# The first input tile of a pooling kernel is loaded by two transfers instead of one

## The chip, the cores and the metric

The kernel runs on one core of a Trainium2 chip. The core has compute engines with instruction streams of their own: VectorE (DVE in the profile), ScalarE (ACT), GpSimd (POOL) and TensorE (PE, not used here), and SyncE (SP), which issues transfers. Transfers are carried out by 16 DMA engines. SBUF is the memory on the core, with 128 partitions; the input and the output lie in the chip's main memory (HBM). The metric is the device time of one execution in microseconds (us).

## The reference

The input is 32 x 256 rows of 4096 float32 numbers. Each row is cut into 256 windows of 16 neighbours, and the output holds the mean of each window:

```python
batch, channels, length = x.shape          # 32, 256, 4096
for i in range(output_size):               # 256
    start = int(i * length / output_size)
    end = int((i + 1) * length / output_size)
    result[:, :, i] = np.mean(x[:, :, start:end], axis=-1)
```

That is 134.2 MB read and 8.4 MB written.

## The kernel before

The 8192 rows are worked through in 16 tiles. A tile gives each of the 128 partitions 4 rows that lie one behind the other in HBM, so 16,384 numbers or 64 KB; a tile is 8.39 MB. For the first 15 tiles partition p owns rows 60p to 60p+59 and takes 4 of them at a time (`x_many`); the last tile has 512 rows of its own, 4 to a partition (`x_last`). Within a tile the numbers of a partition are seen as `cells` = 1024 windows of `window` = 16.

The pool `inpool` has two buffers for the tile `xin`, so tile t+2 goes into the buffer of tile t. `res_many` holds the results of the first 15 tiles, `res_last` those of the last.

For each tile, in this order in the program:

- L66: SP issues the load of the whole tile, one transfer over 128 partitions. It waits until the work on the tile that had this buffer before is done.
- In the last tile only, L68: SP issues the store of `res_many`, 7680 KB, behind the last load. It waits for L80 of tile 14.
- L69: POOL takes the second half of the windows (`m` = 512 of 1024 and up) and adds the upper 8 numbers of each to the lower 8.
- L74: DVE sums the first half of the windows, 16 numbers each.
- L77: DVE sums the second half, 8 numbers each, after L69.
- L80: ACT multiplies the 1024 sums by 1/16 in place.

After the loop, L85 stores `res_last`, 512 KB. Each engine works through its own instructions in program order, and the framework puts in the waits that the data ask for. All transfers, loads and stores, are issued by SP and stand in one queue.

Of the kernel before, what the change touches and what calls it, by code (L numbers as in the profile page):

```python
# [1 line left out]

# [4 lines left out]


@with_exitstack
def kernel(  # L10
    ctx: ExitStack,
    tc: tile.TileContext,
    x: bass.AP,
    output_size: int,
    out: bass.AP,
):

    nc = tc.nc
    F32 = mybir.dt.float32
    X = mybir.AxisListType.X

    batch, channels, length = x.shape
    ob, oc, olen = out.shape
    assert ob == batch and oc == channels and olen == output_size
    assert length % output_size == 0
    window = length // output_size  # L30
    hw = window // 2
    inv_w = 1.0 / float(window)

    P = nc.NUM_PARTITIONS
    R = 4
    rows = batch * channels
    assert rows % (P * R) == 0
    ntiles = rows // (P * R)
    many = (ntiles - 1) * R
    cells = R * output_size  # L40
    m = cells // 2
    cols = R * length

    xr = x.rearrange("b c l -> (b c) l")
    orow = out.rearrange("b c o -> (b c) o")
    x_many = xr[0 : P * many, :].rearrange("(p r) l -> p (r l)", p=P, r=many)
    o_many = orow[0 : P * many, :].rearrange("(p r) o -> p (r o)", p=P, r=many)
    x_last = xr[P * many :, :].rearrange("(p r) l -> p (r l)", p=P, r=R)
    o_last = orow[P * many :, :].rearrange("(p r) o -> p (r o)", p=P, r=R)

    padpool = ctx.enter_context(tc.tile_pool(name="padpool", bufs=1))
    padpool.tile([P, 32], F32, name="pad")
    inpool = ctx.enter_context(tc.tile_pool(name="inpool", bufs=2))
    respool = ctx.enter_context(tc.tile_pool(name="respool", bufs=1))
    res_many = respool.tile([P, (ntiles - 1) * cells], F32, name="res_many")
    res_last = respool.tile([P, cells], F32, name="res_last")

    for t in range(ntiles):
        last = t == ntiles - 1
        xin = inpool.tile([P, cells, window], F32, name="xin")  # L60
        if last:
            res, base, src = res_last, 0, x_last
        else:
            res, base = res_many, t * cells
            src = x_many[:, t * cols : (t + 1) * cols]
        nc.sync.dma_start(out=xin.rearrange("p o w -> p (o w)"), in_=src)  # L66
        if last:
            nc.sync.dma_start(out=o_many, in_=res_many[:, :])  # L68
        nc.gpsimd.tensor_add(  # L69
            out=xin[:, m:cells, 0:hw],  # L70
            in0=xin[:, m:cells, 0:hw],
            in1=xin[:, m:cells, hw:window],
        )
        nc.vector.reduce_sum(  # L74
            out=res[:, base : base + m], in_=xin[:, 0:m, :], axis=X
        )
        nc.vector.reduce_sum(  # L77
            out=res[:, base + m : base + cells], in_=xin[:, m:cells, 0:hw], axis=X
        )
        nc.scalar.mul(  # L80
            out=res[:, base : base + cells],
            in_=res[:, base : base + cells],
            mul=inv_w,
        )
    nc.sync.dma_start(out=o_last, in_=res_last[:, :])  # L85


# [1 line left out]
_INS = ['x', 'output_size']  # L89
_OUTS = [((32, 256, 256), 'float32')]  # L90

_NUMBERS = {'output_size': 256}


# [26 lines left out]
```

## Time and profile before

| | us |
|---|---|
| median of 3 runs | 334.89 (334.88 to 334.91) |
| the profiled execution | 335.07 |
| its span, first to last instruction | 333.3 |
| DVE busy | 209.7 (63%) |
| POOL busy | 139.7 (42%) |
| ACT busy | 18.2 (5%) |
| a load (L66), median from issue to landing | 25.3 |
| the first load, from issue to landing | 21.7 |
| the store of `res_many` (L68), from issue to landing | 23.7 |
| the store of `res_last` (L85), from issue to landing | 4.9 |

The span is what the profile's own rows cover; what lies around it is in the time of the execution but not in the rows. The profile's page gives the busy time of each engine, the packets of the DMA queue, the chain of waits that ended last, and the costliest groups of instructions with the idle time ahead of them and what ended it. The trace can be asked for any stretch of the span: busy time of each engine, the share of the 16 DMA engines, and the rate. In those stretches a DMA packet is counted where it starts, with its whole duration and its bytes; a stretch much shorter than a packet can therefore show a share above 1, or 0 while engines are at work.

### The profile page before, as it was taken

What the parts mean: (1) busy time and instruction counts of PE and PEld (TensorE: products, weight loads), DVE (VectorE), ACT (ScalarE), POOL (GpSimd) and SP (SyncE); (2) the same over time, 40 slices, a digit from 0 to 9 for tenths busy, and PEclk for the clock granted to TensorE, in tenths of its full rate; (3) what the DMA queues carried; (4) which work ended last, traced back from release to release, by engine and by line L of the source; (5) the groups of instructions that cost most, each with busy time, mean ns of one, the idle gap of its engine ahead of it and who ended that gap; (6) DMA issues with size and microseconds to landing.
All of it is one profiled execution on the core that took longest, in us unless ns stands there. A gap on an engine that the chain in (4) does not pass through costs nothing.

```text
span 333.3 us, 158 instructions
## 1 busy us (share of the span) xinstructions
DVE 209.7 (63%) x32; ACT 18.2 (5%) x17; POOL 139.7 (42%) x20
## 2 busy tenths in 40 slices
DVE  0039295693929568392957849294774929487491
ACT  1000101000010100001010100101010010101001
POOL 0027090643709063360907346090724519082460
DMA  9898989999898989899898989899998989898996
GB/s 378 378 503 378 503 378 472 409 401 480 378 503 378 503 378 496 385 433 448 385 496 378 503 378 503 378 472 409 401 480 378 503 378 503 378 496 385 391 442 299
DMA packets 2592, 142.61 MB, mean 428 GB/s; under 512 B 288, under 2 KB 288, under 8 KB 416
## 3 DMA queue, kind: packets, MB, share of 16 engines
q1 hardware_dynamic: 2592, 142.61, 99.1%
HBM read 134.22 MB, written 8.39 MB: 428 GB/s over the span
## 4 chain that ended last, share of the span: by engine, by line
DMA 66%; POOL 18%; DVE 11%; POOLq 3%; issue 0%; ACT 0%; SPq 0%
DMA xin<-in_x_dram 66%; POOL xin L69 18%; DVE res_many L77 9%; POOLq L116 3%; DVE res_last L77 1%; ACT res_last L80 0%; SPq L66 0%; POOLq L69 0%
## 5 line engine op out<-in xcount | busy, mean ns | idle before, releaser
L69 POOL TENSOR_TENSOR xin<-xin 128x4096 f32<-128x4096 f32 x16 | 139.5, 8717 | 182.0 <-DMA xin<-in_x_dram 182.0
L74 DVE TENSOR_REDUCE res_many<-xin 128x512 f32<-128x8192 f32 x15 | 130.3, 8686 | 107.3 <-DMA xin<-in_x_dram 107.3
L77 DVE TENSOR_REDUCE res_many<-xin 128x512 f32<-128x4096 f32 x15 | 66.3, 4420 | 2.5 <-POOL xin L69 2.3
L80 ACT ACTIVATE res_many<-res_many 128x1024 f32<-128x1024 f32 x15 | 15.8, 1056 | 289.6 <-DVE res_many L77 289.6
L74 DVE TENSOR_REDUCE res_last<-xin 128x512 f32<-128x8192 f32 x1 | 8.7, 8685 | 6.7 <-DMA xin<-in_x_dram 6.7
L77 DVE TENSOR_REDUCE res_last<-xin 128x512 f32<-128x4096 f32 x1 | 4.4, 4420 | 0.2 <-POOL xin L69 0.2
L80 ACT ACTIVATE res_last<-res_last 128x1024 f32<-128x1024 f32 x1 | 1.1, 1056 | 18.9 <-DVE res_last L77 18.9
L80 ACT ACT_TABLE_LOAD x1 | 1.3, 1283 | 0.7 <-PEq L102 0.7
L102 POOL MEMSET const-float32-0.0<- 128x1 f32 x1 | 0.1, 98 | 0.2 <-issue 0.2
L102 POOL MEMSET const-bfloat16-1.0<- 128x1 bf16 x1 | 0.1, 101 | 0.0
L102 POOL MEMSET const-uint8-127<- 128x1 uint8 x1 | 0.1, 101 | 0.0
L102 POOL MEMSET const-float32-1.0<- 128x1 f32 x1 | 0.1, 98 | 0.0
## 6 DMA issues: line engine op xcount, KB each, us to landing
out_dram<-res_many SPq DMA_DIRECT2D x1, 7680.0 KB, 23.7
out_dram<-res_last SPq DMA_DIRECT2D x1, 512.0 KB, 4.9
xin<-in_x_dram SPq DMA_DIRECT2D x16, 25.3
```

The source lines that it names most:

```text
L69: nc.gpsimd.tensor_add(out=xin[:, m:cells, 0:hw], in0=xin[:, m:cells, 0:hw], in1=xin[:, m:cells, hw:window],)
L74: nc.vector.reduce_sum(out=res[:, base : base + m], in_=xin[:, 0:m, :], axis=X)
L77: nc.vector.reduce_sum(out=res[:, base + m : base + cells], in_=xin[:, m:cells, 0:hw], axis=X)
L80: nc.scalar.mul(out=res[:, base : base + cells], in_=res[:, base : base + cells], mul=inv_w,)
L102: nc = _bacc.Bacc("TRN2", target_bir_lowering=False, num_devices=1)
L116: with _tile.TileContext(nc) as tc:
```

## The change

The load of the first tile is issued as two transfers, one behind the other on SP: partitions 0 to 15, then partitions 16 to 127. All other tiles keep one transfer over all partitions. Nothing else differs.

```diff
-        nc.sync.dma_start(out=xin.rearrange("p o w -> p (o w)"), in_=src)
+        xflat = xin.rearrange("p o w -> p (o w)")
+        for lo, hi in ((0, 16), (16, P)) if t == 0 else ((0, P),):
+            nc.sync.dma_start(out=xflat[lo:hi, :], in_=src[lo:hi, :])
```

## The prediction

> **What bounds the kernel now.** I read the page first, then the chain of waits, the timeline of the first 62 us, and stretches of the DMA record. The queue's row comes first:
>
> ```profile
> ## 3 DMA queue, kind: packets, MB, share of 16 engines
> q1 hardware_dynamic: 2592, 142.61, 99.1%
> L69 POOL TENSOR_TENSOR xin<-xin 128x4096 f32<-128x4096 f32 x16 | 139.5, 8717 | 182.0 <-DMA xin<-in_x_dram 182.0
> L74 DVE TENSOR_REDUCE res_many<-xin 128x512 f32<-128x8192 f32 x15 | 130.3, 8686 | 107.3 <-DMA xin<-in_x_dram 107.3
> ```
>
> The 16 DMA engines are busy for 99.1% of the span, and both compute engines idle for the input. The packets count themselves: 288 under 512 B are 16 (one per engine, the completion marks) for each of 18 transfers, and the remaining 2304 are 128 for each transfer. So one data packet is one partition's share, 64 KB of input, and with 16 engines each has 8 of them per tile.
>
> ```profile
> 55.05 0.02 issue
> 55.07 25.44 DMA xin<-in_x_dram
> 80.51 0.02 issue
> ```
>
> This piece of the chain, repeated every second tile, is a whole period: the load of tile t+2 is issued when L77 of tile t ends (55.07) and lands 25.44 us later, though the engines need only 19.35 us for a tile. The other 6.1 us are the rest of the load ahead of it, so the queue never runs dry. The stretches say the same:
>
> ```profile
> 2.75:22.10 19.35, 0.00 (x0) 0.00 (x0) 0.00 (x0) 1.00 1.00 434
> 22.10:41.45 19.35, 13.11 (x2) 1.06 (x1) 8.72 (x1) 1.00 1.00 434
> 273.65:293.00 19.35, 13.11 (x2) 1.06 (x1) 8.72 (x1) 1.00 1.00 434
> 312.35:331.70 19.35, 13.11 (x2) 1.06 (x1) 8.72 (x1) 1.00 0.92 395
> ```
>
> In columns: stretch, length, DVE, ACT and POOL busy, clock, DMA share, GB/s. A tile is 8.39 MB in 19.35 us, or 2.42 us per 64 KB packet and engine. The last row shows the queue still moving after the last load: the 7680 KB of `res_many` were issued at 307.51, run behind that load, and land 23.7 us later at 331.2; the last 512 KB, issued at 327.48, run behind them and land at 332.4. The chain of waits names POOL 18% and DVE 11%, but those hide under queued transfers. The end is set by the slowest DMA engine's whole list, so what that engine loses in tile 0 is added to the end one for one.
>
> The start of that list, in stretches of packet starts (GB/s times length, divided by 65,536 bytes, counts them):
>
> ```profile
> 1.60:1.70 0.10, 0.00 (x0) 0.10 (x1) 0.00 (x0) 1.00 0.00 0
> 1.70:1.80 0.10, 0.00 (x0) 0.10 (x1) 0.00 (x0) 1.00 9.91 3277
> 1.80:1.90 0.10, 0.00 (x0) 0.10 (x1) 0.00 (x0) 1.00 8.01 2621
> 1.90:2.90 1.00, 0.00 (x0) 0.11 (x1) 0.00 (x0) 1.00 1.25 459
> 2.90:4.70 1.80, 0.00 (x0) 0.00 (x0) 0.00 (x0) 1.00 0.00 0
> 4.70:5.30 0.60, 0.00 (x0) 0.00 (x0) 0.00 (x0) 1.00 4.03 1748
> 7.10:7.70 0.60, 0.00 (x0) 0.00 (x0) 0.00 (x0) 1.00 4.03 1748
> ```
>
> 5, 4 and 7 engines begin their first packet between 1.7 and 2.9 us, all 16 their second between 4.7 and 5.3, the third between 7.1 and 7.7: lockstep, 2.4 us apart. (A row counts a packet where it starts, so shares exceed 1.)
>
> **The change part by part.** *Issue.* One transfer more on SP, 0.33 us by the median of L66's sixteen, between tile 0's first issue and tile 1's. Tile 1's load then goes out some 0.33 us later, behind 19.35 us of queued work; without that cover it would cost 0.33. Nothing moves on POOL's or ACT's queue, and SP's next entry, tile 2's load, still waits for tile 0's L77.
>
> *Bytes and completion marks.* The bytes are the same. There are 16 more small packets, one per engine. The last packet of a tile and the first of the next stand 2.45 us apart (19.15 to 21.60), others 2.40 to 2.45, so a mark costs 0 to 0.05 us. I take 0.03.
>
> *Waits.* L69 and L74 of tile 0 read partitions of both pieces, so both wait for both transfers; should this take a semaphore instruction of its own, the end's rows of that kind begin at 0.017 us. Behind L69 and L74 stand only tile 0's L77 and L80 and then tile 2's load, which has 6.1 us of cover. Nothing on the end's path.
>
> *Start.* 16 packets, one per engine, could reach all engines sooner than 128. Upper bound of the gain: the second packets spread from 4.70 to 5.25 us, so if all engines ran like the earliest, 0.55 us. Lower bound: nothing, since late starters already catch up (1.0 us of spread becomes 0.55). I take 0.2 us gained.
>
> *The first piece's path.* This is the term that matters, and the trace of before does not price it. Every row shows 16 engines working at once, each through its own eight partitions; it never shows several engines sending to neighbouring partitions, and it cannot say whether 2.42 us belongs to the engine or to the strip of SBUF that it writes. The first piece puts one packet on each engine, all 16 into partitions 0 to 15. Lower bound: the engine is the limit, 2.42 us as now, cost 0. Upper bound: the strip is, with 128/16 = 8 neighbours to a strip: 16 packets in 2 strips, 8 in each, 8 x 2.42 = 19.35 us, cost +16.9. Between 16 paths and 2 I take 4 (the rows show all 16 in use only when all 128 partitions are written, so I lean to the narrow end): 4 rounds, 9.68 us, **+7.26**.
>
> *The second piece's path.* 112 partitions over 16 engines are 7 each, in whatever order. Lower bound: no collision, 7 x 2.42 = 16.9 us, cost 0. Upper bound: every engine always shares a strip with one other, since sevens do not line up with eights: 7 x 4.84 = 33.9, +16.9. I take the middle, half of the seven shared: 3.5 x 2.42 = **+8.47**. There is a floor if strips matter at all and the first piece takes 9.68 us: strips it left idle still owe their whole 8 packets, so tile 0 ends no earlier than 9.68 + 19.35, at least +9.7.
>
> [...]
>
> *Sum.* +0.03 - 0.2 + 7.26 + 8.47 = +15.6 us. On the profiled execution (span 333.3, whole run 335.07, so 1.77 around the span) that is 350.7. The median is 334.89, 0.18 lower, so the prediction is **350.5 us**, 4.7% slower. Compute keeps its cover: tile 0 lands late, tile 1's load lies behind it, and each tile's 13.3 us of work fits its 19.35 as before.
>
> **The rivals.**
>
> *No collision, no change.* The engine is the limit; 16 packets to 16 neighbours take 2.42 us. Then +0.03 - 0.2: 334.7, range 334.2 to 335.0. For it: the even lockstep, as one would see if each engine had its own speed. Against: lockstep also follows if each engine has its own strip, and before never breaks that pairing. Chance 0.20.
>
> *Faster.* The early start is worth more than I grant: all 0.55 us, and the engines' new offsets take away the last load's excess (tile 15 lands at 313.06, tile 14's at 293.09, 19.97 apart against 19.35, 0.6 us): -1.1, 333.8. It would decide only where the first piece costs under 0.5 us, so where no strip matters. For it: the DMA engines set the end, so every tenth saved at the start counts. Against: the stretches are already at 434 GB/s with no idle time to win. Chance 0.08.
>
> *Uneven shares.* The change does not use 16 engines for the short piece but 4, with 4 packets each, while the second still gives 7 to all. Then four engines have 11 packets for tile 0, 3 x 2.42 = +7.26: 342.2. The other twelve run ahead until their buffers stop them, and the end is the four's. For it: nothing in the trace fixes how 16 partitions are dealt out. Against: 128 gave exactly 8 each. Chance 0.06.
>
> *Collision* as forecast: 0.66, from its floor of +9.7 (344.6) to about +22 (357), where nearly all the second piece is shared. If the second piece collided four deep throughout, as the first, it would be 7 x 7.26 = +50.8 and the time about 393; that is in the 0.66, at 0.04, outside the range.
>
> **How the numbers follow.** What this kernel's measurement can tell from no change is about 0.2%, 0.67 us. Faster by more: 0.08; within: 0.20; slower: 0.66 + 0.06 = 0.72. The collision's own range is 344.5 to 357. Without the no-change case over 2 in 10 would be left out, so the range reaches down to 334.4 and holds all but about half of the faster case, the four-deep case and a little at its edges: **334.4 to 357**.
>
> **What would show it.** In the stretches of the DMA record: if 16 packets start by 2 us and the next only after about 11, four paths served the first piece; if the second packets start at 4.7 to 5.3 as now, none collided. Packets of 4.8 us in the stretch after that show the second piece's pairs, and their absence leaves only the floor. The wait of L74 for tile 0, 22.49 us before, should be about 38. From tile 1 on, the period should again be 19.35 us at 434 GB/s, and the loss carried unchanged to the end; a period that changes would make the one-for-one rule wrong. Unequal packet counts per stretch in tile 0 would show uneven shares. The prediction is wrong if tile 0 lands near 22.5.

## The result, and the profile after

The changed kernel takes 355.61 us (median of 4 runs, 355.17 to 356.42) against 334.88: a ratio of 1.062, 95% interval 1.061 to 1.064, so 20.7 us slower. The profiled execution took 355.50 us with a span of 353.7, 20.4 more than before. Lines have moved by two: L68 is the load, L71 POOL's addition, L76 and L79 the sums.

From the page, its head and the rows of the queue and of the compute groups that wait for input:

```profile
span 353.7 us, 161 instructions
DVE 209.7 (59%) x32; ACT 18.2 (5%) x17; POOL 139.7 (39%) x20
DMA packets 2608, 142.61 MB, mean 403 GB/s; under 512 B 304, under 2 KB 304, under 8 KB 432
q1 hardware_dynamic: 2608, 142.61, 98.8%
L71 POOL TENSOR_TENSOR xin<-xin 128x4096 f32<-128x4096 f32 x16 | 139.5, 8718 | 202.4 <-DMA xin<-in_x_dram 202.4
L76 DVE TENSOR_REDUCE res_many<-xin 128x512 f32<-128x8192 f32 x15 | 130.3, 8686 | 128.3 <-DMA xin<-in_x_dram 128.3
```

Compute is the same to 0.1 us. The 16 new packets are under 512 B (304 for 288), the marks of one transfer more; the data packets are as many as before. POOL's wait for input grew by 20.4 us (182.0 to 202.4), as much as the span. The DMA engines still count as 98.8% busy, for the 99.1% of before: they hold as many data packets for longer. The busy share does not show the loss here; the rate does, 403 GB/s for the 428 of before:

```profile
DMA packets 2592, 142.61 MB, mean 428 GB/s; under 512 B 288, under 2 KB 288, under 8 KB 416
```

The timeline has the loss in one place. Here is DVE's first sum of tiles 0, 14 and 15 before:

```profile
22.49 8.69 DVE L74 TENSOR_REDUCE res_many<-xin 128x512 f32<-128x8192 f32 x1 [22.49 <-DMA xin<-in_x_dram]
...
293.11 8.69 DVE L74 TENSOR_REDUCE res_many<-xin 128x512 f32<-128x8192 f32 x1 [6.08 <-DMA xin<-in_x_dram]
313.08 8.69 DVE L74 TENSOR_REDUCE res_last<-xin 128x512 f32<-128x8192 f32 x1 [6.69 <-DMA xin<-in_x_dram]
```

And after, the same sum of tiles 0, 1, 2, 14 and 15:

```profile
43.96 8.69 DVE L76 TENSOR_REDUCE res_many<-xin 128x512 f32<-128x8192 f32 x1 [43.96 <-DMA xin<-in_x_dram]
63.16 8.69 DVE L76 TENSOR_REDUCE res_many<-xin 128x512 f32<-128x8192 f32 x1 [5.99 <-DMA xin<-in_x_dram]
82.45 8.69 DVE L76 TENSOR_REDUCE res_many<-xin 128x512 f32<-128x8192 f32 x1 [6.07 <-DMA xin<-in_x_dram]
...
314.13 8.69 DVE L76 TENSOR_REDUCE res_many<-xin 128x512 f32<-128x8192 f32 x1 [6.09 <-DMA xin<-in_x_dram]
333.46 8.69 DVE L76 TENSOR_REDUCE res_last<-xin 128x512 f32<-128x8192 f32 x1 [6.05 <-DMA xin<-in_x_dram]
```

Tile 0 arrives at 43.96 instead of 22.49, 21.47 us late. After that the period is (314.13 - 43.96) / 14 = 19.30 us, before (293.11 - 22.49) / 14 = 19.33; that returns 0.45 us, and the last tile follows after 19.33 instead of 19.97, which returns 0.64. 21.47 - 1.09 is the 20.4 of the span.

The stretches of the changed kernel at the start (last two columns: DMA share and GB/s; a packet counts where it starts, so rate times length over 65,536 bytes is the number started, and share times length times 16 engines over that number is their mean duration):

```profile
1.60:2.20 0.60, 0.00 (x0) 0.42 (x1) 0.00 (x0) 1.00 14.20 1748
2.20:9.60 7.40, 0.00 (x0) 0.00 (x0) 0.00 (x0) 1.00 0.00 0
9.60:11.10 1.50, 0.00 (x0) 0.00 (x0) 0.00 (x0) 1.00 3.54 699
11.10:15.10 4.00, 0.00 (x0) 0.00 (x0) 0.00 (x0) 1.00 0.00 0
15.10:16.00 0.90, 0.00 (x0) 0.00 (x0) 0.00 (x0) 1.00 5.19 1165
16.00:19.80 3.80, 0.00 (x0) 0.00 (x0) 0.00 (x0) 1.00 0.00 0
19.80:20.70 0.90, 0.00 (x0) 0.00 (x0) 0.00 (x0) 1.00 3.54 1165
```

All 16 engines start in the first row (1748 GB/s x 0.60 us / 65,536 B = 16), and none starts a second packet for 7.4 us. The first packet took 14.20 x 0.60 x 16 / 16 = 8.52 us; the same sum over the first packets of before gives 2.34 x 1.30 = 3.04 (its row stands below). The second takes 3.54 x 1.50 = 5.3, the third 5.19 x 0.90 = 4.67, the fourth 3.19; the further four, by the stretches that follow, 3.7, 4.4, 4.6 and 4.6. From tile 1's second packet on all are 2.42 us again. The first packets before:

```profile
1.60:2.90 1.30, 0.00 (x0) 0.41 (x1) 0.00 (x0) 1.00 2.34 807
```

### The profile page after: what moved, and what is told of

The parts are those of the page before. It is cut to its first block, busy times and chain, and to the rows that moved or that the text cites. A ratio compares the mean times of both kernels' runs of the same rounds, so it can differ in the third digit from the quotient of the medians.

```text
span 353.7 us, 161 instructions
## 1 busy us (share of the span) xinstructions
DVE 209.7 (59%) x32; ACT 18.2 (5%) x17; POOL 139.7 (39%) x20
## 3 DMA queue, kind: packets, MB, share of 16 engines
q1 hardware_dynamic: 2608, 142.61, 98.8%
## 4 chain that ended last, share of the span: by engine, by line
DMA 62%; POOL 20%; DVE 10%; another core or an unknown queue 3%; POOLq 3%; issue 0%; ACT 0%; SPq 0%
DMA xin<-in_x_dram 62%; POOL xin L71 20%; DVE res_many L79 9%; POOLq L118 2%; DVE res_last L79 1%; ACT res_last L82 0%; SPq L68 0%; POOLq L71 0%
## 5 line engine op out<-in xcount | busy, mean ns | idle before, releaser
L71 POOL TENSOR_TENSOR xin<-xin 128x4096 f32<-128x4096 f32 x16 | 139.5, 8718 | 202.4 <-DMA xin<-in_x_dram 202.4
L76 DVE TENSOR_REDUCE res_many<-xin 128x512 f32<-128x8192 f32 x15 | 130.3, 8686 | 128.3 <-DMA xin<-in_x_dram 128.3
L79 DVE TENSOR_REDUCE res_many<-xin 128x512 f32<-128x4096 f32 x15 | 66.3, 4420 | 2.5 <-POOL xin L71 2.3
L76 DVE TENSOR_REDUCE res_last<-xin 128x512 f32<-128x8192 f32 x1 | 8.7, 8686 | 6.0 <-DMA xin<-in_x_dram 6.0
L79 DVE TENSOR_REDUCE res_last<-xin 128x512 f32<-128x4096 f32 x1 | 4.4, 4420 | 0.2 <-POOL xin L71 0.2
## 6 DMA issues: line engine op xcount, KB each, us to landing
xin<-in_x_dram SPq DMA_DIRECT2D x17, 25.3
```

The source lines that it names most:

```text
L71: nc.gpsimd.tensor_add(out=xin[:, m:cells, 0:hw], in0=xin[:, m:cells, 0:hw], in1=xin[:, m:cells, hw:window],)
L76: nc.vector.reduce_sum(out=res[:, base : base + m], in_=xin[:, 0:m, :], axis=X)
L79: nc.vector.reduce_sum(out=res[:, base + m : base + cells], in_=xin[:, m:cells, 0:hw], axis=X)
```

## The experiments

Unless said otherwise, each is one run, set against the median of the kernel before on the same chip. Those medians lie between 334.55 and 335.00 us, and single runs of the kernel before between 334.55 and 335.13, so a few tenths of a microsecond between two experiments mean nothing.

**Where the first piece's price lies.** Four kernels put one more load ahead of tile 0 in the kernel before, into `res_many`, which is written over later. The bytes are the same in all four, 60 KB for each engine; the rows differ, and the first has packets of 7.5 KB instead of 60 KB. DST and SRC stand for columns `0:w` of the partitions named:

```diff
+    w = many * output_size                       # 15360 numbers, 60 KB
+    nc.sync.dma_start(out=DST, in_=SRC)
     for t in range(ntiles):
```

With DST, SRC all 128 partitions of `res_many` and of `x_many`, and an eighth of the columns (`w // 8`):

> The kernel before with one more load ahead of tile 0: 0.98 MB into all 128 partitions of res_many (7.5 KB each; L74 and L77 write over it later, so the output is unchanged). It is the plain price of 60 KB more for each engine, with no engine sharing a destination. Every theory: 60/64 of a 2.42 us packet, +2.3 us, 337.2 us; somewhat more if the smaller packets (7.5 KB) cost something.

With `res_many[0:16]`, `x_many[0:16]`:

> The same bytes, one 60 KB packet on each engine, but into partitions 0 to 15 only, from the 16 rows that the changed kernel's first piece reads. Destination theory (engines that write to neighbouring partitions share a path): 60/64 of the 8.5 us that the changed kernel's first packets took, +8.0 on average and up to +8.7 for the last engine: 342.9 to 343.6. Source theory (the 16 source rows, 0.98 MB apart in HBM, are what collides): the same. Theory that the two-transfer form itself costs: +2.3, 337.2.

With `res_many[0:128:8]`, `x_many[0:16]`:

> As the run with the near destination, the same 16 source rows, but into partitions 0, 8, 16 and so on to 120. Source theory: unchanged, +8.0 to +8.7. Destination theory with strips of eight neighbours: no two engines share, +2.3 (337.2). [...]

With `res_many[0:16]`, `x_many[0:128:8]`:

> As the run with the near destination, into partitions 0 to 15, but from the source rows of partitions 0, 8, 16 and so on to 120, eight times farther apart. Destination theory: as there, +8.0 to +8.7 (343 to 344). Source theory: the collision goes or changes, below +5.

| destination, source | us | over before (334.55) |
|---|---|---|
| all 128, all 128 | 337.07 | +2.52 |
| 0 to 15, rows of 0 to 15 | 342.70 | +8.15 |
| 0, 8, ... 120, rows of 0 to 15 | 339.17 | +4.62 |
| 0 to 15, rows of 0, 8, ... 120 | 343.15 | +8.60 |

The first stretches of the near destination, then of the spaced one:

```profile
1.60:2.40 0.80, 0.00 (x0) 0.00 (x0) 0.00 (x0) 1.00 9.95 1229
2.40:8.80 6.40, 0.00 (x0) 0.00 (x0) 0.00 (x0) 1.00 0.00 0
```

```profile
1.60:2.40 0.80, 0.00 (x0) 0.00 (x0) 0.00 (x0) 1.00 5.79 1229
2.40:5.60 3.20, 0.00 (x0) 0.00 (x0) 0.00 (x0) 1.00 0.00 0
```

The same 16 source rows take 9.95 x 0.80 = 7.96 us a packet into neighbours and 4.63 into every eighth partition. Spacing the source instead leaves the price where it was (+8.60 for +8.15). So the destination decides, and the source theory falls. Strips of eight neighbours, my upper bound in the prediction, fall too: by them every eighth partition would have cost +2.3, and it cost +4.62. The near destination came out near what I had worked from the changed kernel's packets: 7.96 us for 8.0.

**Two transfers as such.** Tile 0 in two transfers of the same sizes, cut by columns (timed over 11 runs):

```diff
+        for lo, hi in ((0, cols // 8), (cols // 8, cols)) if t == 0 else ((0, cols),):
+            nc.sync.dma_start(out=xflat[:, lo:hi], in_=src[:, lo:hi])
```

> Tile 0 in two transfers cut the other way: all 128 partitions, the first eighth of the columns (8 KB each), then the rest (56 KB). Same bytes in each transfer as in the change. Destination theory: no engine leaves its own partitions, so no collision: 334.4 to 335.1, within 0.2% of before, with 16 small packets more and perhaps 0.2 us won or lost at the start. If two transfers as such cost what the change cost: near 355.

Measured 334.95 us against 334.93, ratio 1.0001 (0.9992 to 1.001). The second issue, the 16 marks and the second wait come to nothing that shows (+0.02 us). (The start is not that of the changed kernel: here 128 packets of 8 KB go first.) The cut through the partitions makes the loss: 355.61 us with it, 334.95 with the cut by columns.

**The second piece alone.**

```diff
+        if t == 0:
+            nc.vector.memset(xflat[0:16, :], 0.0)
-        for lo, hi in ((0, 16), (16, P)) if t == 0 else ((0, P),):
+        for lo, hi in ((16, P),) if t == 0 else ((0, P),):
```

> The changed kernel without its first piece: partitions 0 to 15 of tile 0 are set to zero by DVE instead of loaded, so their results for tile 0 are left out. One packet less for each engine. If the second piece collides as the changed kernel's packet durations say (second to eighth packets 5.3, 4.67, 3.2, 3.7, 4.4, 4.6, 4.6 us on average, 30.5 in all, 13.6 above 7 x 2.42), then 13.6 less the missing packet's 2.42: +11, about 346. If the second piece only suffered from engines thrown out of step by the first: 7 x 2.42, so -2.4, 332.

Measured 345.95, +11.0, although each engine has one packet less (this kernel leaves out partitions 0 to 15 of tile 0). Its first stretches:

```profile
1.60:2.60 1.00, 0.00 (x0) 0.42 (x1) 0.00 (x0) 1.00 4.30 1049
2.60:5.50 2.90, 1.29 (x1) 0.00 (x0) 0.00 (x0) 1.00 0.00 0
5.50:7.60 2.10, 2.10 (x1) 0.00 (x0) 0.00 (x0) 1.00 2.21 499
7.60:10.30 2.70, 2.70 (x1) 0.00 (x0) 0.00 (x0) 1.00 0.00 0
```

The very first packets take 4.30 us and the next 2.21 x 2.10 = 4.64. The seven rounds have the changed kernel's pattern (4.3, 4.6, 3.1, 3.9, 4.5, 4.6, 4.6). So the first piece did not throw the engines out of step: 112 partitions collide by themselves, +11.0 and the missing 2.42, 13.4 us in all.

**Two halves.**

```diff
-        for lo, hi in ((0, 16), (16, P)) if t == 0 else ((0, P),):
+        for lo, hi in ((0, 64), (64, P)) if t == 0 else ((0, P),):
```

> Tile 0 in two transfers of 64 partitions, 0 to 63 and 64 to 127, 4 rows for each engine. [...] Engine-only: 334.7.

Measured 355.71, +20.8. The stretch 6.40 to 7.90 us of this kernel:

```profile
6.40:7.90 1.50, 0.00 (x0) 0.00 (x0) 0.00 (x0) 1.00 3.42 699
```

All 16 second packets take 3.42 x 1.50 = 5.13 us, and so do nearly all of tile 0's other seven (means of the rounds 4.9 to 5.13). That is 2.12 times the 2.42 us of a whole load; two engines at one destination the whole time would give 2 x 2.42 = 4.84 by my estimate, but no row shows which engines meet. The engine-only time, 334.7, is out.

**Another place in the queue.** The split at tile 6 (`if t == 6`):

> The same two-transfer load for tile 6 instead of tile 0, when the queue has been running for over 100 us. If the loss is the collision of packets and passes to the end one for one: +19 to +21, 354 to 356. If it needs the idle start, or if buffered tiles absorb part of it: below +15.

Measured 357.66, +22.7, a little over the range. L76 of this kernel, tiles 5 to 7:

```profile
120.81 8.69 DVE L76 TENSOR_REDUCE res_many<-xin 128x512 f32<-128x8192 f32 x1 [7.45 <-DMA xin<-in_x_dram]
...
162.01 8.69 DVE L76 TENSOR_REDUCE res_many<-xin 128x512 f32<-128x8192 f32 x1 [27.92 <-DMA xin<-in_x_dram]
...
181.22 8.69 DVE L76 TENSOR_REDUCE res_many<-xin 128x512 f32<-128x8192 f32 x1 [5.98 <-DMA xin<-in_x_dram]
```

Tile 6 follows tile 5 after 41.2 us, 21.9 more than a period, and tile 7 after 19.2. DVE's wait rises from 6 to 27.9: two buffers absorb nothing, since the queue itself is the limit. Tile 5 is late too, by about 1.4 us (its wait is 7.45); that its last engines are held up when the others begin the first piece is likely, but not shown. The loss needs neither the idle start nor a place at the head of the queue.

**Which sixteen partitions.** Every eighth partition cost +4.62, all 128 +2.52 for the same bytes. And the second piece's rounds differ among themselves: alone, 4.64 us a packet in the second and 3.1 in the third. No row shows which engines' destinations meet, so four more extra loads of 60 KB a row as above, with SRC `x_many[0:16]`, try other sets of 16:

DST `res_many[11:117:7]`:

> The extra 60 KB packet on each engine, 16 rows into partitions 11, 18, 25 and so on to 116 (every seventh). [...]

DST `res_many[16:122:7]`:

> The same with partitions 16, 23, 30 and so on to 121, which are the first rows of the second piece if engine e has rows 16+7e to 22+7e. [...]

DST `res_many[18:124:7]`:

> The same with partitions 18, 25, 32 and so on to 123, the third rows of the second piece by that dealing, where the changed kernel's packets took 3.2 us on average. [...]

DST `res_many[28:89:4]`, another step, so partitions 28, 32, 36 and so on to 88 (timed over 4 runs):

> [...] If the step of seven itself mattered: below 338.

Measured: every seventh partition from 11 337.69 (+2.69, before 335.00), from 16 338.87 (+3.87), from 18 339.66 (+4.66); every fourth from 28 339.74 (+4.98, before 334.76; ratio 1.0147, 1.013 to 1.0164). At one step of seven the price is +2.69 or +4.66 by where the set starts, and a step of four does not bring it below 338: the step alone does not set it. From 11 the packets of the extra load took 3.48 x 0.90 = 3.13 us, about as long as the first packets of the kernel before (64 KB), 3.04:

```profile
1.60:2.50 0.90, 0.00 (x0) 0.00 (x0) 0.00 (x0) 1.00 3.48 1092
```

One stretch compares the runs, 5 to 6 us, in which tile 0's packets start on the engines that are through; first from 11, then from 16, then every fourth from 28:

```profile
5.00:6.00 1.00, 0.00 (x0) 0.00 (x0) 0.00 (x0) 1.00 2.56 1049
```

```profile
5.00:6.00 1.00, 0.00 (x0) 0.00 (x0) 0.00 (x0) 1.00 0.40 131
```

```profile
5.00:6.00 1.00, 0.00 (x0) 0.00 (x0) 0.00 (x0) 1.00 2.59 852
```

At 65.5 KB a packet: 16 engines are through from 11, 2 from 16, 13 from 28. From 16 the other fourteen follow by 7.15 us, so nearly all are held up, and the end is 3.87 us later than before; from 28 most are not, but the last of the three others goes on only at 7.9, and the end is 4.98 us later.

The second piece itself shows both, without the start's delay. Its second round, the changed kernel's third packet, took 4.67 us on average; alone, its 16 packets took 4.3 to 4.8 us each. Its third round is the changed kernel's fourth packet, which all 16 engines begin between 19.8 and 20.7 us. Their next packets:

```profile
23.00:23.50 0.50, 0.00 (x0) 0.00 (x0) 0.00 (x0) 1.00 6.55 1835
23.50:25.00 1.50, 0.00 (x0) 0.00 (x0) 0.00 (x0) 1.00 0.00 0
25.00:25.30 0.30, 0.00 (x0) 0.00 (x0) 0.00 (x0) 1.00 1.51 437
```

Fourteen engines go on at 23.0 to 23.5 and exactly two at 25.0 to 25.3: about 4.8 us for two, and with the mean of 3.19 about 2.96 for the fourteen, 0.5 above 2.42. So one round slows two engines by much and the round before slows all 16; which destinations do the one and which the other, no run shows.

## Why the prediction was right, and where its sizes were off

*The bound, and one for one.* Right: the delay is made in tile 0 and carried to the end, less 1.09 us. The period stayed at 19.30. DVE's wait for tile 0, forecast at about 38 us, was 43.96. I had not counted that the last load would lose its 0.64 us excess.

*Issue, marks, waits, start.* I summed -0.17; the cut by columns, which has the second issue, the marks and the second wait, measured +0.02 within an interval of 0.3 either way. Right, and too small to be seen. The start did come sooner, all 16 engines by 2.2 us instead of 2.9, but no run shows whether it is worth the 0.2 us. The "faster" rival is out at 355.61 us.

*The first piece, +7.26.* Right mechanism, a little dear. Four paths were a choice between two bounds that no row of before decides, and no run counts paths; that the number came out near was luck. The first packets took 8.52 us, not 4 x 2.42 = 9.68. By the near and the spread extra load the piece costs 342.70 - 337.07 = 5.6 us for 60 KB, 6.0 for 64 KB. Its 1.05 MB went in between 1.75 and 11.0 us, first packet's start to last packet's end: 113 GB/s, against 434 in a whole load.

*The second piece, +8.47.* This is the step that was mis-sized: "the middle, half of the seven shared". Alone it measures 13.4 us, nearer to the upper bound of 16.9. I took half of the seven packets at 4.84 us and half at 2.42; in five of the seven rounds the mean was 4.3 to 4.6 us, and in the other two 3.1 and 3.9 (second piece alone). The upper bound's reason, that every engine always shares, does not fit the third round either, where fourteen engines needed about 2.96 us. Together the two pieces by themselves make 6.0 + 13.4 = 19.4 of the 20.7. The remaining 1.3, no more than the changed kernel's runs differ among themselves (355.17 to 356.42), likely lie where one piece's last packets meet the next one's first, which I had not counted: the second piece's first packets took 5.3 us behind the first piece and 4.30 alone. The first piece's 1.3 too much hid as much of the second's 4.9 too little, so the total is a little nearer than its terms; 355.61 lies near the top of the range.

*The rivals.* No change is out at 355.61 us, and by the halves' 355.71: the engine's own speed is not the only limit. Uneven shares are out: 16 packets start in the first stretch, and an engine starts one at a time (before has 128 queued for tile 0, and 16 start by 2.9 us). Four-deep collision throughout is out: the second piece alone costs 13.4, not 50.8.

*What stays open:* why one round slows all 16 engines by some 2.2 us a packet, and the next two engines by 2.4 and the others by 0.5. Every one-packet run here has the start's own delay in it (first packets of 3.04 us before, 2.42 later); a long transfer with the same set of 16 partitions in every round was not tried. Which rows go to which engine no run shows, since no row names partitions and engines together; so the dealing with 16+7e, where an expectation uses it, was an assumption, and the prediction's "each through its own eight partitions" is inferred as well. No version tried is faster than the kernel before.

## What to carry to other kernels

When all DMA engines are the bound, as here at 99.1%, leave the partition range of a load whole: in a load of all 128 every packet but the first took 2.42 us, and both cuts through them that were tried, 16 and 112 or two halves, cost over 20 us on a load of 19.35. Cut by columns if two transfers are wanted; that was free here (334.95 us for 334.93). A DMA share near 99% says nothing against such a loss (98.8% with it, 99.1% without); compare the duration of one packet, or GB/s, between stretches.

## What was not expected of the hardware

The loss does not come in whole rounds of 2.42 us. An engine moved its 64 KB in 2.42 us in a load of all 128 partitions (27.1 GB/s), in 5.13 us in the halves (12.8 GB/s, 2.12 times as long) and in 8.52 us in the first piece (7.7 GB/s, 3.52 times). And a piece of 16 partitions need not be slow: every seventh partition from 11 cost +2.69, within 0.2 us of the same bytes over all 128 (+2.52).
